# DeltaNet preparation by pairs of heads, in a new order of its parts, with the rotation's swapped rows copied inside SBUF

## The chip, the cores and the metric

The kernel runs on one NeuronCore of a Trainium2 chip. The metric is the device time of one execution in microseconds (us); the kernel before took 1733.33 us (median of 3 runs, 1732.29 to 1735.43).

## The reference: what is computed

One layer of a hybrid encoder is applied, with the same parameters, to a prompt of 1024 tokens and a sample of 256 tokens (1280 together, model width 1024). The normalized tokens are projected once (`h @ w_in`), and the columns go to two groups of heads:

```python
def _layer(...):
    h = _rmsnorm(x, norm_mix_pre)
    qkv_a, z_a, b_f, b_b, a_f, a_b, q_b, k_b, v_b = _split_cols(h @ w_in)
    o_a = _gated_deltanet(...)   # conv of 5 taps + SiLU, unit q/k, chunked delta rule, forward and backward
    o_b = _axial_gqa(...)        # per-head RMS norm of q/k, axial rotation, softmax attention
    x = x + _rmsnorm(concat([o_a, o_b]) @ w_out, norm_mix_post)
    f = square(relu(_rmsnorm(x, norm_mlp_pre) @ w_up)) @ w_down
    return x + _rmsnorm(f, norm_mlp_post)
```

For every chunk the delta rule solves a unit lower triangular system whose matrix is made of products of keys, a decay and a gate (`tri = I + strict(kk)`, `triangular_solve(tri, [v_beta, k_beta*exp(gc)])`). The kernel forms the inverses of these matrices itself, for 4 heads, 10 chunks of 128 tokens and 2 directions. In the attention group 4 query heads and 2 key heads are normalized and rotated (`x1*c - x2*s, x1*s + x2*c` on halves of 32 rows); 2 value heads aren't.

## The kernel before, in words

The program has four stages: norm and the z projection; the **preparation** of all heads; the scan over chunks together with attention; output projection and MLP. The change lies in the preparation. Each engine works in its own program order: PE (matmul), DVE, ACT, POOL, and SP, which here only issues DMAs.

The preparation is written as generators, one per part and head, and the string `ORDER` (L39 to L43) says which is advanced next; `next(parts[step_], None)` runs it to its next `yield` (L634 to L637). A scheduler then arranges the instructions of each engine by their place in this order and by what they depend on, and pools of buffers add dependences: a tile of a pool of one buffer can be written only when the readers of the tile before are done.

The parts are:

- **K** (`gdn_qk`): for one head the k projection and convolution, 10 transposes of k (`kt`, L459) of which ACT takes sums of squares and two scaled copies (`kn`, L464), and the same for q (`qt`, L473, without the copies). A projection (`proj_T`) is 72 matmuls `pt`: three for each of 8 slices of the depth (high by high, low by high, high by low; L367 to L369) over column groups of 512, 512 and 256 tokens. The convolution (`conv_proj`) has two steps on ACT, three long ones on DVE (L443), one on POOL (L444), a tanh on ACT (L445) and a last step on DVE (L446). The transposes need that last step.
- **V** (`gdn_v`): the same for v, with transposes `vt` (L502).
- **E** (`gdn_e`): for two chunks at a time, gate differences are built on PE in `pe` (L516, L522) from a tile `ER`, for direction 0 on POOL and for direction 1 on DVE (both L518); ACT takes the exponential `E` (L523); products of keys with keys and queries land in `pk` (L528), and DVE forms `A` (L529) and the system's matrix `C` (L531).
- **S** (`gdn_sub`): the 32x32 diagonal blocks of `C` are copied out (`Cc`, ACT L545), transposed (L547), written to DRAM and read back so that each of 80 partitions holds one block (`Rm`), which is inverted by 31 steps of elimination: a product `prod` (DVE L560), a sum into `Rm` (DVE L561), a memset (POOL L562). Once for each head.
- **L** (`gdn_lev`): `Rm` goes to DRAM (`r_d`, L569) and comes back as `Rc`; from the blocks' inverses the inverses of 64 and 128 rows are assembled in two levels of small matmuls with copies between (32x32: `ph` L589, `py` L596, `px` L601; 64x64: `ph` L618, `py` L625). The result is stored in `vis_d` (L629, L630), from where the scan loads it (`vis`, L652).
- **a** (`att_proj`): a projection of attention into `araw`. For q and k (a0 to a5) it is written to DRAM (`aqkv_d`, L391) and read back with its blocks of 32 rows swapped (`axw`, L394); 10 transposes (`at`, L400) give the sums of squares on ACT (`gj`, L376) for the norm; DVE multiplies `araw` and `axw` by the tables (L415, L416), POOL adds them (L417), and for a4 and a5 the keys are scaled by `prk`, a product on PE (L423, L426). The result goes to `arot_d` (L430). a6 and a7 are the values (`avn`, L406, L407). Attention reads `arot_d` as `ax` (L663).

In PSUM the preparation has eight banks: 3 for projections (`pt`), 2 shared by `pe` and `pk`, 1 for `kt`, `qt` and `vt`, 1 for the levels, and 1 for `at` and `prk`. The scan's first matmuls are `ps_s` (attention, L712) and `p` (L810).

## Time and profile before

| what | us |
|---|---|
| median of 3 runs (lowest to highest) | 1733.33 (1732.29 to 1735.43) |
| the profiled execution's own time | 1735.97 |
| span of its trace | 1734.2 |
| PE busy in it | 1622.7 (94%) |
| DVE, ACT, POOL busy | 1284.9, 851.7, 737.2 |
| start of attention's first product `ps_s`, of the scan's first `p` | 537.23, 541.73 |

The span is what the profiler recorded of one execution, 1.8 us less than that execution's own time. A row of waits names the instruction that waited, the one it waited for, the total, how often, and the longest. A row of instruction groups has the line, the engine, out<-in, the shapes and the count, then busy time and the mean length of one; behind the last bar stands the engine's idle time just ahead of the group. Where instructions overlap in an engine's pipeline, busy time divided by the count is less than the mean length. A row by windows gives busy time (and count) of each engine in a stretch of the span, then the granted clock of PE. The `order` rows below give only the sequence on one engine and say nothing of time.

### The profile page before, as it was taken

The page shows a single profiled execution, that of the slowest core. Times are in us where ns is not written, and L with a number is a line of the kernel's source. Part 1 is how long each engine was busy: PE and PEld are TensorE (multiplying, and loading weights), DVE is VectorE, ACT ScalarE, POOL GpSimd, SP SyncE. Part 2 cuts the span into 40 slices and gives each one's busy share as a digit, 9 for nine tenths or more (in the row PEclk, how much of TensorE's full clock was granted, in tenths as well). Part 3 has the DMA queues.
Part 4 walks back from the last instruction along what each step waited for, and adds up shares of the span by engine and source line. Part 5 has one row for each costly group of instructions (what it writes and reads, how often), then busy time and mean ns, then how long its engine had stood idle before and what let it go on. Part 6 is the DMA issues. An engine that isn't in the chain of part 4 may idle for free. (4 is left out here: it accounts for less than half of the span.)

```text
span 1734.2 us, 27996 instructions
## 1 busy us (share of the span) xinstructions
PE 1622.7 (94%) x9799; PEld 1386.8 (80%) x9799; DVE 1284.9 (74%) x2551; ACT 851.7 (49%) x1937; POOL 737.2 (43%) x656
## 2 busy tenths in 40 slices
PE   5999898988997999889998999999998999999997
PEld 4877676767775888658877999999988888888885
DVE  7545798997655788885659759555797878888777
ACT  4326566654344767674436546544554333333412
POOL 3212241312113434440103634644647677788762
PEclk9999999999998999999999999999999999999999
DMA  6213334545547866244334445444655444444234
GB/s 199 80 31 112 100 109 119 155 114 151 156 126 222 290 197 211 80 155 154 117 109 131 160 140 174 150 133 137 220 189 197 150 147 148 134 134 143 86 120 151
DMA packets 208779, 252.68 MB, mean 146 GB/s; under 512 B 35073, under 2 KB 163391, under 8 KB 208639
## 3 DMA queue, kind: packets, MB, share of 16 engines
q1 hardware_dynamic: 208495, 250.77, 45.8%
q8 instruction: 77, 1.26, 0.3%
q14 instruction: 63, 0.52, 0.1%
q0 software_dynamic: 144, 0.13, 0.0%
HBM read 159.75 MB, written 91.10 MB: 145 GB/s over the span
## 5 line engine op out<-in xcount | busy, mean ns | idle before, releaser
L1161 PE MATMUL pd<-mh,uhl 128*128 128x320 f32 x892 | 278.0, 312 | 6.8 <-DVE uhl L1152 6.7
L1160 PE MATMUL pd<-mh,uhl 128*128 128x320 f32 x892 | 276.5, 311 | 2.1 <-ACT uhl L1151 1.9
L1162 PE MATMUL pd<-ml,uhl 128*128 128x320 f32 x892 | 276.7, 310 | 0.0
L1304 DVE TENSOR_TENSOR acc<-acc,pd 128x512 f32<-128x512 f32 x330 | 207.0, 679 | 44.8 <-PE pd L1300 44.8
L1298 PE MATMUL pd<-dhi,fhi 128*128 128x512 f32 x490 | 193.0, 394 | 4.3 <-DVE acc L1306 4.3
L1299 PE MATMUL pd<-dl,fhi 128*128 128x512 f32 x490 | 192.8, 394 | 0.0
L1300 PE MATMUL pd<-dhi,flo 128*128 128x512 f32 x490 | 192.4, 393 | 0.0
L367 PE MATMUL pt<-h_hi,whi 128*128 128x512 f32 (+1 forms) x480 | 178.7, 372 | 0.0
L369 PE MATMUL pt<-h_hi,wlo 128*128 128x512 f32 (+1 forms) x480 | 178.4, 372 | 0.0
L368 PE MATMUL pt<-h_lo,whi 128*128 128x512 f32 (+1 forms) x480 | 178.2, 371 | 0.0
L1161 PEld LDWEIGHTS pd<-mh,uhl 128*128 128x128 f32 x892 | 168.8, 189 | 9.5 <-DVE uhl L1152 9.5
L1160 PEld LDWEIGHTS pd<-mh,uhl 128*128 128x128 f32 x892 | 168.5, 189 | 3.8 <-ACT uhl L1151 3.8
L1162 PEld LDWEIGHTS pd<-ml,uhl 128*128 128x128 f32 x892 | 168.6, 189 | 0.0
L1280 ACT CAST fhi<-fr 128x1280 fp32r<-128x1280 f32 x49 | 62.1, 1268 | 206.7 <-PE pd L1299 119.0
L80 POOL TENSOR_TENSOR dl<-dw,dhi 128x1024 fp32r<-128x1024 f32 x49 | 128.4, 2620 | 53.8 <-ACT dhi L79 53.3
L1205 POOL TENSOR_TENSOR s<-u,u 128x320 f32<-128x320 f32 x32 | 29.3, 915 | 224.4 <-ACT u L1170 219.5
L1152 DVE TENSOR_TENSOR uhl<-us,uhl 128x512 fp32r<-128x512 f32 x88 | 93.4, 1062 | 37.8 <-ACT uhl L1151 36.9
L727 POOL TENSOR_TENSOR P<-P,sm 128x512 f32<-128x512 f32 (+1 forms) x72 | 73.5, 1042 | 94.9 <-DVE sm L725 40.4
L1298 PEld LDWEIGHTS pd<-dhi,fhi 128*128 128x128 f32 x490 | 92.4, 188 | 25.8 <-DVE acc L1306 4.7
L1300 PEld LDWEIGHTS pd<-dhi,flo 128*128 128x128 f32 x490 | 92.3, 188 | 20.8
L1299 PEld LDWEIGHTS pd<-dl,fhi 128*128 128x128 f32 x490 | 92.4, 189 | 20.5
L1169 ACT ACTIVATE u<-u 128x320 f32<-128x320 f32 x128 | 60.1, 470 | 90.8 <-DVE u L1186 37.3
(359 smaller groups left out, 4128.5 us busy)
## 6 DMA issues: line engine op xcount, KB each, us to landing
fr<-r_d SPq DMA_DIRECT2D x49, 640.0 KB, 4.0
vis<-vis_d SPq DMA_DIRECT2D x64, 384.0 KB, 4.2
uraw<-in_w_up SPq DMA_DIRECT2D x22, 1024.0 KB, 5.4
r_d<-s SPq DMA_DIRECT2D x128, 160.0 KB, 1.8
r_d<-u SPq DMA_DIRECT2D x96, 160.0 KB, 1.9
dw<-in_w_down SPq DMA_DIRECT2D x28, 512.0 KB, 5.0
wraw<-in_w_in SPq DMA_DIRECT2D x48, 256.0 KB, 3.4
x<-in_x_prompt SPq DMA_DIRECT2D x16, 512.0 KB, 3.4
```

The source lines that it names most:

```text
L80: (V if leng is None else leng).tensor_tensor(lo, src, f32(hi), ALU.subtract)
L367: T.matmul(pm[:, :n], lhsT=whi, rhs=h_hi[:, k, t0:t0 + n], start=(k == 0), stop=False)
L368: T.matmul(pm[:, :n], lhsT=whi, rhs=h_lo[:, k, t0:t0 + n], start=False, stop=False)
L369: T.matmul(pm[:, :n], lhsT=wlo, rhs=h_hi[:, k, t0:t0 + n], start=False, stop=(k == KD - 1))
L1152: V.tensor_tensor(lo, ua[n][UP[i][0]], f32(hi), ALU.subtract)
L1160: T.matmul(pm, lhsT=w[0][:, k], rhs=mh[b, i][:, k], start=(k == 0), stop=False)
L1161: T.matmul(pm, lhsT=w[1][:, k], rhs=mh[b, i][:, k], start=False, stop=False)
L1162: T.matmul(pm, lhsT=w[0][:, k], rhs=ml[b, i][:, k], start=False, stop=(k == 3))
L1298: T.matmul(pm, lhsT=r[0][:, k, tk], rhs=w[0][:, k], start=(k == 0), stop=False)
L1299: T.matmul(pm, lhsT=r[0][:, k, tk], rhs=w[1][:, k], start=False, stop=False)
L1300: T.matmul(pm, lhsT=r[1][:, k, tk], rhs=w[0][:, k], start=False, stop=(k == Q - 1))
L1304: V.tensor_tensor(half(t, d), half(t, d), pm, ALU.add)
```

## The change

It has six parts, all in the preparation.

1. `ORDER` is another string. V0's projection stands behind K0's; the values a6 and a7 come early; a4 and a5 run while the second pair is eliminated; the levels L2 stand among a0 and a1 and L3 at the very end. There are more `yield`s in K, V, `att_proj` and S, so that the parts can be cut finer; in K the q projection comes before k's convolution.
2. S works on **two heads at once**: `Rm` is [80, 2, 32, 32], and each of the 31 steps has one product, one sum and one memset for both heads. `Rm` and `prod` have one buffer of double size each.
3. `ER` of direction 0 is four ACT copies with a scale instead of one POOL operation; `ER` and `A` have two buffers instead of one.
4. The PSUM banks of the transposes, levels, `at`, `prk` and now also `pk` are one shared pool `fx` of 3; `pe` keeps its 2 banks alone.
5. The swapped rows of `araw` are copied from SBUF to SBUF by four DMAs; the trip through `aqkv_d` goes. `axw` lies in the halves of a tile of the `qk` pool (two buffers), beside the tables in the other, so that both wait for K2's and K3's `qk` to be released.
6. `Cc` shares its buffer with `Rt`.

The diff, cut to its core:

```diff
 ORDER = (
-    "K0 K0 K0 K0 E0 E0 E0 E0 K1 E0 K1 S0 K1 K1 L0 E1 E1 V0 V0 E1 E1 L0 E1 K2 K2 K2 K2 E2 E2 E2 V1 E2 E2 "
...
-    "a2 a2 a3 a3 a7 a7"
+    "K0 K0 K0 V0 K0 K0 V0 E0 K1 E0 V0 E0 E0 K1 E0 K1 a6 K1 K1 a6 E1 E1 V1 E1 E1 E1 S0 K2 S0 V1 S0 K2 S0 V1 S0 K2 "
...
+    "V3 S1 a4 S1 a5 S1 a4 a5 a0 a5 L2 a0 a1 L2 a0 a1 a2 a1 a2 a3 a2 L3 a3 L3 a3"
...
-    tq_tile = b_tile("tq", 1)
-    iv_tile = b_tile("iv", 1)
-    at_tile = b_tile("at", 1)
+    tq_tile = iv_tile = at_tile = b_tile("fx", 3)
...
-            SP.dma_start(out=aqkv_d[j], in_=raw)
-            xw = tp_.tile([128, TOK], F32, tag="cy", name="axw", bufs=1)
+            xw = att["xw"][:, j % 2, 0:TOK]
             for b in range(4):
-                SP.dma_start(out=xw[b * 32:b * 32 + 32], in_=aqkv_d[j][(b ^ 1) * 32:(b ^ 1) * 32 + 32])
+                SP.dma_start(out=xw[b * 32:b * 32 + 32], in_=raw[(b ^ 1) * 32:(b ^ 1) * 32 + 32])
...
-    yield from conv_proj(4 + h, qk[:, 1])
+    pk_, pq_ = conv_proj(4 + h, qk[:, 1]), conv_proj(h, qk[:, 0])
+    next(pk_)
+    yield
+    next(pq_)
+    next(pk_, None)
+    yield
...
-                R = gp.tile([128, 2, 2, 128], F32R, tag="ER", name="ER", bufs=1)
-                (G if d == 0 else V).tensor_tensor(
...
+                R = gp.tile([128, 2, 2, 128], F32R, tag="ER", name="ER", bufs=2)
...
+                if d == 0:
+                    for i in range(2):
+                        for j in range(2):
+                            S.activation(R[:, i, j], incl[:, d], AF.Copy, scale=gd[:, i, j:j + 1])
...
-                pk = tr_tile("pk")
+                pk = tq_tile("pk")
...
-        Rm = gp.tile([80, 32, 32], F32, tag="Rm", name="Rm", bufs=2)
...
+        Rm = gp.tile([80, 2, 32, 32], F32, tag="Rm", name="Rm", bufs=1)
...
+            prod = gp.tile([80, 2, 256], F32, tag="prod", name="prod", bufs=1)
+            pv = prod[:, :, :p * n].rearrange("q h (j c) -> q h j c", j=p)
+            V.tensor_tensor(pv, Rm[:, :, p, 0:p][:, :, :, None].to_broadcast([80, 2, p, n]),
+                            Rm[:, :, p:p + 1, p:].to_broadcast([80, 2, p, n]), ALU.mult)
+            V.tensor_tensor(Rm[:, :, 0:p, p:], Rm[:, :, 0:p, p:], pv, ALU.add)
+            G.memset(Rm[:, :, p, 0:p], 0.0)
+            if p % 5 == 0:
+                yield
```

Three places show what this does to the sequence. The first is PE while E2 and E3 are built. In the kernel before, around the first group of E2 (`pe_2772`), with `pt` a projection's matmuls (the number behind a name is a buffer's):

```order
L516 MATMUL pe_2772<-nmask_839,identr_837 128x256
L522 MATMUL pe_2772<-ER_2774,strict_835 128x256 x2
L516 MATMUL pe_2772<-nmask_839,identr_837 128x256
L368 MATMUL pt_3754<-h_lo_100,whi_3744 128x512
L528 MATMUL pk_2785<-qk_2409 128x256
L459 MATMUL kt_3443<-ident_110,qk_3148 128x128 x2
L369 MATMUL pt_3754<-h_hi_99,wlo_3745 128x512
L522 MATMUL pe_2772<-ER_2779,strict_835 128x256 x2
```

and in the changed kernel, inside E2 and E3:

```order
L539 MATMUL pk_3591<-qk_2346 128x256
L533 MATMUL pe_3696<-ER_3706,strict_829 128x256
L539 MATMUL pk_3596<-qk_2346 128x256
L478 MATMUL qt_3603<-ident_104,qk_2843 128x128 x4
L522 MATMUL pe_3816<-nmask_833,identr_831 128x256
L533 MATMUL pe_3816<-ER_3818,strict_829 128x256 x2
L522 MATMUL pe_3816<-nmask_833,identr_831 128x256
L533 MATMUL pe_3816<-ER_3826,strict_829 128x256 x2
L478 MATMUL qt_3616<-ident_104,qk_2843 128x128 x4
L478 MATMUL qt_3629<-ident_104,qk_2843 128x128 x2
L539 MATMUL pk_3682<-qk_2346 128x256
```

Before, projections' matmuls stand between the parts of a group. Now, from `pk_3553` (six rows ahead of these) to the `at` transposes of a4, five groups of `pe`, 14 `pk` and 10 `qt` stand without a single `pt` between them. K3's `kt` have moved ahead of this, behind the levels of heads 0 and 1; one more group of `pe` and 30 `pt` stand between those and this place.

The second place is DVE where the rotated keys are scaled (`prk`), here of the first of a4 and a5. In the kernel before:

```order
L529 TENSOR_TENSOR A<-E,pk 128x256
L531 SCALAR_TENSOR_TENSOR C<-pk,sca,E 128x128 x2
L426 TENSOR_TENSOR araw<-araw,prk 128x512
L80 TENSOR_TENSOR wlo<-wraw,whi 128x512
L426 TENSOR_TENSOR araw<-araw,prk 128x512
L547 STREAM_TRANSPOSE Ct<-Cc 128x320
L426 TENSOR_TENSOR araw<-araw,prk 128x256
L415 SCALAR_TENSOR_TENSOR araw<-araw,nw,rope 128x1024
```

and in the changed one, where `80x2x...` is a step of the elimination of heads 2 and 3:

```order
L99 SCALAR_TENSOR_TENSOR rsa<-nat,nay 128x10
L575 TENSOR_TENSOR prod<-Rm 80x2x231
L577 TENSOR_TENSOR Rm<-Rm,prod 80x2x11x21
L425 TENSOR_TENSOR araw<-araw,prk 128x512
L575 TENSOR_TENSOR prod<-Rm 80x2x220
L425 TENSOR_TENSOR araw<-araw,prk 128x512
L577 TENSOR_TENSOR Rm<-Rm,prod 80x2x10x22
L425 TENSOR_TENSOR araw<-araw,prk 128x256
L575 TENSOR_TENSOR prod<-Rm 80x2x207
L415 SCALAR_TENSOR_TENSOR axw<-axw,nw,rope 128x1024
```

Before, E's operations were the neighbours, and the elimination of head 3 came later (`Ct`, which leads up to it, stands here). Now the norms and rotations of a4 and a5 lie between the steps of the elimination of heads 2 and 3, with one of its operations ahead of nearly each of theirs.

The third place is the end of the preparation. On PE before, with the last projection (a7), its transposes and attention's first products:

```order
L368 MATMUL pt<-h_lo,whi 128x256
L369 MATMUL pt<-h_hi,wlo 128x256
L400 MATMUL at<-ident,araw 128x128 x10
L712 MATMUL ps_s<-k_hi,q_hi 128x512
L713 MATMUL ps_s<-k_lo,q_hi 128x512
L714 MATMUL ps_s<-k_hi,q_lo 128x512
```

and in the changed kernel, behind a3's projection and the 32x32 levels of head 3:

```order
L398 MATMUL at<-ident,araw 128x128 x10
L634 MATMUL ph_5615<-X_1011,C 64x64 x10
L634 MATMUL ph_5627<-X_1011,C 64x64 x10
L641 MATMUL py_5639<-C,H_5614 64x64 x10
L641 MATMUL py_5652<-C,H_5614 64x64 x10
L826 MATMUL p_5839<-vis 128x128 x2
L833 MATMUL p_5845<-vt,vis 128x128 x2
L826 MATMUL p_5854<-vis 128x128 x2
L842 MATMUL p_5845<-vt,vis 128x128 x2
L833 MATMUL p_5860<-vt,vis 128x128 x2
L728 MATMUL ps_s<-k_hi,q_hi 128x512
L729 MATMUL ps_s<-k_lo,q_hi 128x512
```

On SP before:

```order
L407 DMA arot_d<-avn 128x512
L407 DMA arot_d<-avn 128x256
L663 DMA ax<-arot_d 128x256
L663 DMA ax<-arot_d 128x512
L430 DMA arot_d<-araw 128x1280
L652 DMA vis<-vis_d 128x512
L652 DMA vis<-vis_d 128x384
```

and in the changed kernel (the last `arot_d<-araw` is a3's rotation, `vis_d<-C` are head 3's inverses):

```order
L429 DMA arot_d<-araw 128x1280
L679 DMA ax<-arot_d 128x512
L645 DMA vis_d<-C 1280x1x128
L646 DMA vis_d<-C 1280x1x128
L429 DMA arot_d<-araw 128x1280
L668 DMA vis<-vis_d 128x512
L668 DMA vis<-vis_d 128x384
L668 DMA vis<-vis_d 128x128
```

Before, all levels were done ahead of the last projections (L3's matmuls had 36 `pt` among them), and the last work was a7's transposes. Now the levels of head 3 and the norm and rotation of a3 stand behind the last projection with no `pt` left; the scan's loads `vis` stand behind both on SP's queue, and on PE the scan's `p` stands ahead of attention's `ps_s`. L2 stands in the same way, without a `pt` among its matmuls, between a2's projection and a3's.

More of the change, by code (lines that the diff above doesn't have):

```diff
@@ L111, in build @@
     z_d = dr.tile([TOK, 512], F32, name="z_d")
-    aqkv_d = [dr.tile([128, TOK], F32, name=f"aqkv{j}_d") for j in range(6)]
     arot_d = [dr.tile([128, TOK], F32, name=f"arot{j}_d") for j in range(8)]
@@ L380, in att_proj @@
     def att_proj(j):
-        if not att:
+        if not att and j < 6:
             rope = gp.tile([128, 2, 1282], F32, tag="qk", name="rope", bufs=2)[:, :, 0:1024]
             SP.dma_start(out=rope, in_=I["c_rope"])
-            att[0] = rope
-        rope = att[0]
+            att["rope"] = rope
+            att["xw"] = gp.tile([128, 2, 1282], F32, tag="qk", name="axw", bufs=2)
+        rope = att.get("rope")
         c = (2064 + j * 128, 2576 + (j - 4) * 128, 2832 + (j - 6) * 128)[max(0, j - 2) // 2]
@@ L467, in gdn_qk @@
         yield
-        yield from conv_proj(h, qk[:, 0])
+        next(pq_, None)
+        yield
         for t0 in range(0, NT, 4):
@@ L496, in gdn_v @@
         yield from conv_proj(8 + h, vT)
+        yield
         irk = irks[h]
@@ L537, in gdn_e, with gdn_sub @@
         Cs[h] = C
[L539 to L555 removed]
+    def gdn_sub(pair):
+        Rm = gp.tile([80, 2, 32, 32], F32, tag="Rm", name="Rm", bufs=1)
+        for i in range(2):
+            h = 2 * pair + i
+            C = Cs[h]
+            Cc = gp.tile([128, 2, NT, 32], F32, tag="Rt", name="Cc", bufs=1)
+            for b in range(4):
+                bs = slice(32 * b, 32 * b + 32)
+                S.mul(Cc[bs], C[bs, :, :, bs].rearrange("p t d c -> p d t c"), -1.0)
+            Ct = gp.tile([128, NT, 32], F32, tag="Ct", name="Ct", bufs=1)
+            V.transpose(Ct.rearrange("p t c -> p (t c)"), Cc[:, 0].rearrange("p t c -> p (t c)"))
+            c_d = dr.tile([128, 2, NT, 32], F32, tag="c_d", name="c_d", bufs=2)
+            SP.dma_start(out=c_d[:, 0], in_=Ct)
+            SP.dma_start(out=c_d[:, 1], in_=Cc[:, 1])
+            for b in range(4):
+                SP.dma_start(out=Rm[20 * b:20 * b + 20, i], in_=c_d[32 * b:32 * b + 32].rearrange("j d t i -> (d t) j i"))
+            Rms[h] = Rm[:, i]
+        G.memset(Rm.rearrange("p h a b -> p h (a b)")[:, :, 0:1024:33], 1.0)
+        yield
```

31 lines of the change are left out of this document (6 added, 25 removed), and 1 row of the table ORDER.

## The prediction

> **What bounds the kernel now.** I first read the busy shares of the profile's first part: PE is busy for 94% of the span, but the change touches only the preparation, so what counts is read there. The table of windows cuts that stage by time; its columns are each engine's busy time, then the granted PE clock:
>
> ```profile
> core 0: us, PE busy (x) PEld busy (x) DVE busy (x) ACT busy (x) POOL busy (x), PEclk, DMA share, GB/s
> 112.00:212.00 100.00, 88.90 (x459) 72.28 (x460) 62.78 (x111) 60.07 (x170) 24.54 (x29) 0.98 0.37 102
> 212.00:312.00 100.00, 91.97 (x719) 74.13 (x719) 87.52 (x187) 66.37 (x177) 27.79 (x70) 0.95 0.45 121
> 312.00:392.00 80.00, 71.50 (x621) 56.83 (x620) 77.12 (x180) 43.29 (x114) 21.81 (x52) 1.00 0.46 124
> 392.00:492.00 100.00, 92.23 (x736) 74.75 (x735) 70.19 (x191) 40.21 (x131) 19.47 (x45) 0.97 0.49 140
> 492.00:542.00 50.00, 40.45 (x434) 31.80 (x433) 19.01 (x52) 16.96 (x48) 7.12 (x3) 0.83 0.58 177
> 501.00:509.00 8.00, 8.00 (x98) 6.61 (x96) 1.12 (x3) 2.48 (x5) 0.00 (x0) 0.57 0.01 2
> 532.00:542.00 10.00, 4.64 (x11) 3.24 (x12) 3.44 (x7) 1.97 (x4) 1.27 (x1) 0.50 0.93 302
> ```
>
> PE is the engine that sets the pace. The first five rows cover 430 us, PE is busy in 385.05 of them, and so idles 44.95. DVE is nearly its equal only from 312 to 392 (77.12 of 80). What a new order can win is this idle time, so I next asked what PE waited for, by its waits in the first 280 us and in the rest:
>
> ```profile
> PE vt L502 <- DVE vT L446: 7.1, 3, 2.5
> PE pe L516 <- DVE C L531: 5.9, 5, 2.5
> PE qt L473 <- DVE qk L446: 3.6, 2, 2.2
> PE pk L528 <- DVE prod L560: 2.3, 1, 2.3
> PE kt L459 <- DVE qk L446: 1.9, 1, 1.9
> ```
>
> ```profile
> PE ps_s L712 <- ACT q_hi L79: 6.2, 1, 6.2
> PE prk L423 <- DVE araw L426: 4.1, 2, 2.6
> PE pe L516 <- DVE C L531: 2.3, 1, 2.3
> PE prk L423 <- DVE rsa L98: 0.8, 1, 0.8
> ```
>
> Each `vt`, `qt` or `kt` waits because its transposes stand close behind a convolution that isn't done; each `pe` waits for a bank whose last user was a `pk` that DVE still had to read.
>
> **The change part by part.** (a) *Waits that go.* Transposes now stand a projection or more behind their convolution, and `pk` leaves the two banks of `pe`. That addresses 7.1 + 3.6 + 1.9 = 12.6 us and 5.9 + 2.3 = 8.2 us, with the 2.3 of `pk` 23.1 in all. Not all stays won: K3's `kt` and its neighbours share three banks with everything else, and each reader there can be late in the same way. I count 18 us won, with ends at 23 (nothing replaced) and 12 (half replaced).
>
> (b) *Elimination by pairs.* The rows of its products and sums:
>
> ```profile
> L561 DVE TENSOR_TENSOR Rm<-Rm,prod 80x31 f32<-80x31 f32 (+15 forms) x124 | 51.6, 416 | 2.3
> L560 DVE TENSOR_TENSOR prod<-Rm 80x31 f32<-80x31 f32 (+15 forms) x124 | 43.4, 350 | 4.0 <-POOL Rm L555 1.9
> L560 DVE TENSOR_TENSOR prod<-Rm 80x31 f32<-80x31 f32 x8 | 1.5, 183 | 2.0 <-POOL Rm L555 1.9
> L560 DVE TENSOR_TENSOR prod<-Rm 80x256 f32<-80x256 f32 x4 | 1.7, 418 | 0.1
> ```
>
> From 31 to 256 elements the product grows from 183 to 418 ns, 1.04 ns for an element, which leaves 183 - 32 = 151 ns that don't depend on size. 248 operations become 124 of twice the size, so 124 x 151 ns = 18.7 us of DVE go, of 95.0. The Trainium skill, page "Perfetto Trace Analysis", section "Optimizing Scalar/DVE Operations", puts the overhead of a DVE operation on SBUF at about 60 ns of engine time and says that the profiled latency is about twice that, since half overlaps with the next instruction; by it 124 x 60 ns = 7.4 us would go, an estimate. The rows' 151 ns are over twice that; each step here needs the one before, so little of a step can overlap, and the sum keeps to the rows.
>
> What does it bring PE? Where PE waits for something else, nothing. Only from 312 to 392 is DVE nearly full, and PE idles there for 80 - 71.50 = 8.5 us. So the gain lies between 0 and 8.5; I take 3, near zero, because no elimination step is among what PE waits for, but for the single 2.3 us already used.
>
> (c) *The stretch of E2 and E3 with no projection in it* (first place of the order). The rows that price it:
>
> ```profile
> L518 POOL TENSOR_TENSOR ER<-incl,gr 128x512 fp32r<-128x512 f32 x20 | 29.3, 1463 | 70.6 <-PE pe L522 70.6
> L518 DVE TENSOR_TENSOR ER<-incl,gr 128x512 fp32r<-128x512 f32 x20 | 15.6, 782 | 9.4 <-PE pe L522 9.3
> L464 ACT ACTIVATE kn<-kt,cum 128x128 f32<-128x128 f32 x80 | 22.6, 397 | 0.2 <-DMA vis_d<-kn 0.2
> L523 ACT ACTIVATE E<-pe 128x512 f32<-128x512 f32 x20 | 12.1, 603 | 18.1 <-PE pe L522 18.1
> L529 DVE TENSOR_TENSOR A<-E,pk 128x256 f32<-128x256 f32 x40 | 16.5, 412 | 12.4 <-ACT E L523 7.7 <-PE pk L528 2.6 <-ACT cy L440 2.1
> L531 DVE SCALAR_TENSOR_TENSOR C<-pk,sca,E 128x128 f32<-128x128 f32 x80 | 24.3, 341 | 0.4 <-DMA vis_d<-C 0.4
> L516 PE MATMUL pe<-nmask,identr 128*128 128x256 f32 x40 | 12.9, 322 | 8.3 <-DVE C L531 8.2
> L522 PE MATMUL pe<-ER,strict 128*128 128x256 f32 x80 | 18.1, 307 | 1.4 <-DVE ER L518 1.4
> L528 PE MATMUL pk<-qk 128*128 128x256 f32 x80 | 26.1, 413 | 3.2 <-DVE prod L560 2.3 <-ACT E L523 0.7
> L473 PE MATMUL qt<-ident,qk 128*128 128x128 f32 x40 | 7.3, 299 | 4.4 <-DVE qk L446 3.6 <-ACT gj L376 0.6
> ```
>
> A scaled copy of 128x128 on ACT takes 22.6 / 80 = 0.28 us where they run back to back (`kn`). So the four for one `ER` cost 1.13 us, and POOL loses 29.3 us of work that delayed no one by more than 1.4. PE's own work in the stretch is 10 x 0.32 + 20 x 0.226 + 14 x 0.326 + 10 x 0.18 = 14.1 us. DVE's is 5 x 0.78 + 14 x (0.41 + 2 x 0.30) = 18.1 us. A group taken serially is 1.13 (copies) + 0.45 (PE) + 0.78 (DVE's `ER`) + 0.45 (PE) + 0.60 (`E`) + 0.41 (`pk`) + 1.09 (`A`, two `C`) = 4.9 us, and five are 24.5. The exposed idle time is then between 18.1 - 14.1 = 4 and 24.5 - 14.1 = 10 us, up to 14 with the sixth group ahead of it, which has 30 short `pt` as cover. I take 10: two banks of `pe`, and `ER`, `A` and `C` of neighbouring groups queued on one DVE, are nearer to the serial end.
>
> (d) *The rotations of a4 and a5 between elimination steps* (second place). By the slope of (b) a step of 252 elements for two heads takes 151 + 504 x 1.04 = 675 ns. From a4's sums to its `prk` about eleven steps stand between, 7.4 us, and as much again for a5; `prk` needs `rsa`, and PE works in order, so the projection behind `prk` waits for it too. Before, this place cost 4.1 + 0.8 = 4.9. The ends are -4.9 (the projection ahead covers all) and 2 x 7.4 - 4.9 = +9.9; I take +6: only 24 and 32 `pt` stand between the transposes and `prk`, and at 0.11 us from start to start for 256 columns (the first two rows of the last fence of this part) and twice that for 512, they cover 3 to 7 us of each wait that also holds the sums, the norm and the `wlo` of other projections. The swap inside SBUF is costed at nothing:
>
> ```profile
> L416 DVE SCALAR_TENSOR_TENSOR axw<-axw,nw,rope 128x1024 f32<-128x1024 f32 (+1 forms) x12 | 10.2, 878 | 3.7 <-DMA axw<-aqkv_d 3.7
> ```
>
> The round trip was waited for once, 3.7 us, by DVE and not by PE; that is the most it gives back. Its copies now also wait for K2's and K3's `qk` to be free; behind them on SP stand the loads `wraw` of the next projection. If these come late they cost PE what the rotation costs, so (d)'s upper end holds that too. One buffer each for `Rm` and `prod`, and `Cc` in `Rt`'s, are costed at nothing: steps on DVE follow each other anyway, and L0 and L1 have read the first pair's `Rm` before the second is loaded; were they late, S1 would wait and with it (e).
>
> (e) *L2 with no projection among its matmuls* and (f) *the end*. The levels' first and last matmuls and the stores behind them:
>
> ```profile
> L589 PE MATMUL ph<-Rt,C x160: 191/191/212, 287.2 to 496.1; 32*32 32x32 f32 x160
> L625 PE MATMUL py<-C,H x160: 218/218/268, 297.0 to 512.3; 64*64 64x64 f32 x160
> L629 SPq DMA_DIRECT2D vis_d<-C x4: 523/542/1029, 301.4 to 513.5; - x4
> ```
>
> ```profile
> 527.78 0.28 PE L368 MATMUL pt<-h_lo,whi 128*128 128x256 f32 x1
> 527.89 0.28 PE L369 MATMUL pt<-h_hi,wlo 128*128 128x256 f32 x1
> ...
> 530.63 0.44 PE L400 MATMUL at<-ident,araw 128*128 128x128 f32 x2 [0.68 <-ACT avn L406]
> 537.23 0.80 PE L712 MATMUL ps_s<-k_hi,q_hi 128*128 128x512 f32 x1 [6.17 <-ACT q_hi L79]
> 541.73 0.85 PE L810 MATMUL p<-vis 128*128 128x128 f32 x4
> ```
>
> Head 0 takes 301.4 - 287.2 = 14.2 us from its first level matmul to its store; head 3, from its last first-level matmul to its store, 513.5 - 496.1 = 17.4. In between lie copies on ACT and DVE, for which PE now has nothing to do. For L2 I take 5 us of idle (a third of 14.2; ends 2 and 9, that is half of 17.4). At the end, before, `ps_s` starts 6.2 us late and `p` 541.73 - 531.07 = 10.7 after the last transposes. Now L3's chain of 14.2 to 17.4 stands there, and a store and load through SP behind it, behind a3's rotation on the same queue; against this, L3 no longer stands in the middle, where at a clock of 0.57 the 8 us from 501 to 509 lost 8 x 0.43 = 3.4. The ends are 14.2 - 10.7 - 3.4 = 0 and 17.4 - 10.7 = 6.7 with half as much again for the rotation and the loads behind it, 10; I take their middle, +5.
>
> The sum against the profiled execution is -18 - 3 + 10 + 6 + 5 + 5 = +5 us, 1735.97 + 5 = 1741. That execution lay 2.6 us above the median, so in the measure of the median it is 1733.3 + 5 = 1738.
>
> **The rivals.** About 0.2%, 3.5 us, is what a measurement of this kernel can tell from no change.
>
> *Faster.* The waits of (a) go in full (-23), DVE's saving is worth PE's idle time where DVE is full (-8.5), and the shared banks let PE take matmuls from elsewhere, so that (c) costs 4; with (d), (e) and (f) at half, 8, that is -19.5, or 1714. For it speaks that 23.1 of 45 us idle lie in waits that the order takes apart; against it, that the order shows no cover in (c), (e) and (f). It decides if the stretch of E2 and E3 shows less than about 5 us of PE waits. Chance 0.28.
>
> *No change.* Half of (a) comes back at the shared banks (-12), and (c) to (f) cost as much: 1733. The profile would then show about 45 us of PE idle time, in other rows. Chance 0.15.
>
> *Slower by much.* PE's clock falls where PE waits. The last two rows of windows show it at 0.57 and 0.50, the second behind a wait of 6.2. Through the stretch of (c), at half clock, PE's 14.1 us of work take up to 14.1 more; nearly all of it counts if PE is the serial link there, little if it idles anyway. With the sum's +5 that gives +18, about 1752. It decides from a granted clock below about 0.7 in that stretch. Chance 0.15. The Trainium skill, page "TensorE: Matmul & The Clock Gate", section "Part 1: The HAM clock gate", says that an idle window of about 3.4 us puts PE back to half clock, and as long a busy one lifts it; the trace agrees at 532 to 542 (0.50 behind 6.2 us), and the rule speaks against any order that gathers waits in one place.
>
> **How the numbers follow.** The forecast of 1738 has the remaining chance of 0.42; its terms' ends, taken as independent (half-widths of about 5.5, 4, 5, 7, 3.5 and 5), give about 13 either way, 1725 to 1751. The range reaches a little past the faster rival's 1714, to 1712, and to the slower one's 1752. Faster by over 0.2%: 0.28 and 0.08 of the forecast's lower part, 0.36. Within: 0.13 of the no-change case and 0.07 of the forecast, 0.20. Slower: 0.27 of the forecast, 0.15, and 0.02 of the rest, 0.44.
>
> **What would show it.** Step (a) is right if the waits of `vt`, `qt` and `kt` for L446 fall from 12.6 to under 6 us and `pe` waits for `C` no more. (b): the 124 operations sum to 95.0 - 18.7 = 76 us. (c): a stretch of 25 us or so without `pt`, in which PE is busy for about 14 and waits for ACT or DVE. (d): `prk` or the projection around it waits over 10 us. (e), (f): L2's and L3's matmuls show waits for copies, and the first `p` starts 14 us or more after the last `pt` with head 3's stores just ahead. The forecast is wrong if `p` starts earlier than in the kernel before, at 541.73, by more than 3.5 us, or later by more than 15.

## The result, and the profile after

The changed kernel takes 1752.85 us (median; 1750.26 to 1755.26) against 1732.81 of the kernel before beside it: a ratio of 1.0115, interval 1.0095 to 1.0135, so 20 us slower. The profiled execution took 1753.38 with a span of 1751.6 (before 1735.97 and 1734.2). The forecast was 1738 and slower by 5; the time lies just above the range's 1752.

Read as before, the busy shares first, and then the windows (busy time of each engine, then the granted clock):

```profile
PE 1620.2 (92%) x9799; PEld 1394.0 (80%) x9799; DVE 1257.9 (72%) x2427; ACT 868.5 (50%) x2017; POOL 697.1 (40%) x572
```

```profile
112.00:212.00 100.00, 99.26 (x538) 83.91 (x537) 61.77 (x115) 74.08 (x220) 15.05 (x21) 0.98 0.42 116
212.00:312.00 100.00, 93.64 (x499) 78.17 (x498) 83.22 (x131) 60.71 (x151) 20.93 (x43) 0.98 0.36 97
312.00:392.00 80.00, 69.90 (x848) 55.63 (x847) 48.41 (x114) 47.18 (x137) 3.65 (x10) 0.96 0.47 124
392.00:492.00 100.00, 76.44 (x593) 62.87 (x591) 66.25 (x143) 33.45 (x99) 12.71 (x35) 0.91 0.39 105
492.00:542.00 50.00, 35.25 (x477) 30.00 (x473) 31.78 (x86) 27.22 (x109) 10.95 (x4) 0.77 0.47 131
373.00:398.00 25.00, 18.01 (x84) 12.88 (x85) 19.77 (x70) 19.93 (x67) 0.00 (x0) 0.93 0.70 203
```

The first three stages got better: PE idles 0.74 + 6.36 + 10.10 = 17.2 us there, where it idled 11.1 + 8.03 + 8.5 = 27.6. The gain of 10.4 is then given back and more: from 392 to 542 PE idles 23.56 + 14.75 = 38.3, against 7.77 + 9.55 = 17.3, at a lower clock (0.91 and 0.77, before 0.97 and 0.83). So the question is what happened behind 392. PE's waits from 100 to 570 us (total, times, longest):

```profile
PE at L398 <- DVE araw L425: 11.2, 1, 11.2
PE p L826 <- DMA vis<-vis_d: 11.1, 2, 10.3
PE at L398 <- ACT araw L368: 4.2, 1, 4.2
PE pk L539 <- DVE C L542: 4.0, 2, 3.2
PE px L617 <- issue: 3.8, 3, 1.6
PE pt L365 <- ACT araw L368: 3.7, 1, 3.7
...
PE qt L478 <- DVE qk L445: 2.2, 1, 2.2
...
PE prk L422 <- DVE rsa L99: 1.7, 1, 1.7
PE vt L508 <- DVE vT L445: 1.7, 1, 1.7
```

The waits of the early stages (`vt`, `qt`, `kt`, `pe` for `C`) have all but gone. The two largest are new: one wait of 11.2 us while the second pair is eliminated, one of 10.3 at the scan's first product. Both, and the waits near the first, on PE's timeline (start, duration, and in brackets the idle time ahead with what ended it):

```profile
444.96 2.78 PE L398 MATMUL at<-ident,araw 128*128 128x128 f32 x10 [11.22 <-DVE araw L425]
451.41 0.80 PE L365 MATMUL pt<-h_hi,whi 128*128 128x512 f32 x1 [3.67 <-ACT araw L368]
...
463.26 2.50 PE L422 MATMUL prk<-ident,rsa 128*128 128x128 f32 x20 [1.72 <-DVE rsa L99]
...
546.54 0.77 PE L826 MATMUL p<-vis 128*128 128x128 f32 x2 [10.34 <-DMA vis<-vis_d]
...
553.06 0.55 PE L728 MATMUL ps_s<-k_hi,q_hi 128*128 128x512 f32 x1
```

And DVE's timeline ahead of it:

```profile
415.37 0.69 DVE L81 TENSOR_TENSOR wlo<-wraw,whi 128x512 fp32r<-128x512 f32 x1 [4.06 <-ACT whi L80]
416.79 0.69 DVE L81 TENSOR_TENSOR wlo<-wraw,whi 128x512 fp32r<-128x512 f32 x1 [0.72 <-ACT whi L80]
424.19 0.17 DVE L89 TENSOR_SCALAR nax<-ssa 128x10 f32<-128x10 f32 x1 [6.71 <-ACT gj L374]
...
426.53 0.17 DVE L99 SCALAR_TENSOR_TENSOR rsa<-nat,nay 128x10 f32<-128x10 f32 x1
426.80 0.22 DVE L575 TENSOR_TENSOR prod<-Rm 80x62 f32<-80x62 f32 x1
...
435.60 1.27 DVE L414 SCALAR_TENSOR_TENSOR araw<-araw,nw,rope 128x1024 f32<-128x1024 f32 x1
...
441.09 3.22 DVE L577 TENSOR_TENSOR Rm<-Rm,prod 80x480 f32<-80x480 f32 x1
444.23 0.67 DVE L425 TENSOR_TENSOR araw<-araw,prk 128x512 f32<-128x512 f32 x1
```

Here a4's norm (L89 to L99) stands *ahead* of the second elimination in DVE's program. It waits 6.71 us for the squares that ACT sums from a4's transposes. Only when it is done does the elimination start, at 426.80. a4's rotation (from L414 on) then stands in turn behind and between elimination steps, and the scaling by `prk` (L425), which frees the bank that a5's transposes (`at`) want, comes at 444.23, behind POOL's add for this rotation (440.62 to 443.79, shown in the last section) and the step at 441.09.

### The profile page after: what moved, and what is told of

It reads as the page before. It is cut to its first block, busy times and chain, and to the rows that moved or that the text cites. A ratio compares the mean times of both kernels' runs of the same rounds, so it can differ in the third digit from the quotient of the medians.

```text
span 1751.6 us, 27869 instructions
## 1 busy us (share of the span) xinstructions
PE 1620.2 (92%) x9799; PEld 1394.0 (80%) x9799; DVE 1257.9 (72%) x2427; ACT 868.5 (50%) x2017; POOL 697.1 (40%) x572
## 5 line engine op out<-in xcount | busy, mean ns | idle before, releaser
L1177 PEld LDWEIGHTS pd<-mh,uhl 128*128 128x128 f32 x892 | 168.3, 189 | 11.3 <-DVE uhl L1168 11.2
L367 PE MATMUL pt<-h_hi,wlo 128*128 128x512 f32 (+1 forms) x480 | 174.4, 364 | 0.9 <-DVE wlo L81 0.9
L81 POOL TENSOR_TENSOR dl<-dw,dhi 128x1024 fp32r<-128x1024 f32 x49 | 128.6, 2624 | 54.4 <-ACT dhi L80 53.8
L365 PEld LDWEIGHTS pt<-h_hi,whi 128*128 128x128 f32 x480 | 92.0, 192 | 18.1 <-ACT araw L368 4.1
```

Source lines behind the costliest of these rows:

```text
L81: (V if leng is None else leng).tensor_tensor(lo, src, f32(hi), ALU.subtract)
L365: T.matmul(pm[:, :n], lhsT=whi, rhs=h_hi[:, k, t0:t0 + n], start=(k == 0), stop=False)
L367: T.matmul(pm[:, :n], lhsT=wlo, rhs=h_hi[:, k, t0:t0 + n], start=False, stop=(k == KD - 1))
L1177: T.matmul(pm, lhsT=w[1][:, k], rhs=mh[b, i][:, k], start=False, stop=False)
```

## Experiments

Two events mark how far the late part is: the start of attention (first `ps_s`) and of the scan (first `p`). The last projection matmul (`pt`) starts at 522.1 in the changed kernel and at 527.9 before, but then the changed kernel still has levels of head 3 to do, and the kernel before hasn't; `ps_s` starts at 553.1 against 537.2, and `p` at 546.5 against 541.7. The first matmul of the next stage (`pd`) starts at 923.5 against 907.6, 15.9 later; the spans differ by 17.4.

Before the runs are compared, one thing has to be known. The scheduler arranges the whole program anew for each edit, so PE's order can also turn in the stage of scan and attention, which no edit touches. By the sequence of names on PE from the earlier of the two marks to the first `pd`, the versions fall into groups with the very same sequence, and the time from that mark to `pd` goes with the group (versions by the headings below):

| PE's order in this stage | first | us from the earlier mark to `pd` |
|---|---|---|
| kernel before; "elimination first"; "L3 still last" | `ps_s` | 370.3; 369.6; 370.1 |
| changed kernel; `ER` back on POOL; `Rc` on POOL's queue; the same with "elimination first" | `p` | 376.9; 377.2; 377.0; 378.5 |
| old sequence; late part reordered; a3's store on POOL's queue | `ps_s` | 377.2; 377.1; 379.4 |
| the three with L3 among the projections | `ps_s` | 378.1; 379.0; 378.7 |
| third buffer with step 10 and own banks; with step 18 and `Rc` on POOL's queue | `ps_s` | 378.0; 377.3 |
| third buffer with step 18; elimination head by head | `ps_s` | 385.1; 387.5 |

The three versions that are left have orders of their own: 372.5 (third buffer with step 10), 383.8 (`at` in its own banks) and 376.6 (the kernel before with `ER` on ACT). `ps_s` starts 14 to 24 us ahead of `p` in the last group and with own banks, and 4 to 13 in the other versions where it is first. So a difference between two runs is the price of what was edited only where this order is the same in both. Each trace is of one execution, and some lie off the median: that of own banks took 1752.88, that of `Rc` on POOL's queue 1760.92, that with the third buffer besides 1734.63.

**The old sequence with the new operations.** The string is cut as the new parts need it, in the order of the kernel before:

```diff
-    "K0 K0 K0 V0 K0 K0 V0 E0 K1 E0 V0 E0 E0 K1 E0 K1 a6 K1 K1 a6 E1 E1 V1 E1 E1 E1 S0 K2 S0 V1 S0 K2 S0 V1 S0 K2 "
+    "K0 K0 K0 K0 K0 E0 E0 E0 E0 K1 E0 K1 K1 K1 K1 E1 E1 V0 V0 V0 E1 E1 E1 S0 S0 S0 S0 K2 S0 S0 S0 S0 L0 K2 K2 L0 "
...
```

> All new parts (pairs, ER on ACT, shared banks, copies inside SBUF), but put in the sequence of the kernel before: each part's extra yields are run through at once, the values a6 stand among E3, a7 last, L2 and L3 ahead of a2 and a3. Theory 'late order' (the loss of 20 us lies in the rotations among the elimination, L2 without a projection, and the end, which are matters of the order): 1725 to 1740 us, with the waits of vt, qt and kt for the convolution back (over 8 us in all). Rival 'parts' (the new forms of the operations themselves cost the 20 us): about 1750, whatever the order.

Measured: 1766.87 (1.0186, 1.0159 to 1.0214), slower than either theory said. PE waits 16.6 us for `wlo` and 13.5 for the `at` bank. So the new sequence is not the loss as a whole: with these operations it is 14 us better than this version of the old one.

**`at` in banks of its own** (those of `pe`; only a6 and a7 keep the shared ones):

```diff
-            tp = at_tile("at")
+            tp = (tr_tile if j < 6 else at_tile)("at")
```

> The changed kernel with one edit: the transposes at of a0 to a5 go to the two banks of pe instead of the shared three, so that prk can no longer hold the banks they need. Theory 'banks': the waits of at for DVE L425 (11.2 us) and behind it go and the levels of head 2 find projections between: 1732 to 1743. Rival 'elimination sets the end' (the second elimination ends on DVE at 477.5 and everything behind L2 waits for it): PE only waits later, 1748 to 1753.

Measured: 1746.82 (1.007, 1.0047 to 1.0092), 6 less, between the two expectations. PE's waits show where they went:

```profile
PE ph L605 <- DVE Rt L592: 12.9, 3, 12.5
PE prk L422 <- DVE araw L425: 10.4, 1, 10.4
```

The wait of `at` is gone; the next instruction that needs DVE waits 10.4 instead, and the levels of head 3 another 12.5. In this trace the bank only chose who waits for DVE.

**Elimination head by head**, where the pair stands:

```diff
-            V.tensor_tensor(pv, Rm[:, :, p, 0:p][:, :, :, None].to_broadcast([80, 2, p, n]),
...
+            for i in range(2):
+                R1 = Rm[:, i]
...
```

> The changed kernel with the elimination of the two heads of a pair one after the other (248 operations of single size on DVE instead of 124 of double size); Rm, loads and yields as in the changed kernel. The prediction's reading (pairing is worth 3 us, at most 8.5): 1753 to 1761. Rival 'elimination sets the end' (the second pair's 62 steps lie on the critical path): 9 us more for the second pair alone, 1762 or above. A shift below 1753 would mean that pairing does not help where it stands.

Measured: 1763.06 (1.0166, 1.014 to 1.0192), about 10 us over the changed kernel and in the rival's window. But the last product of the second elimination starts only 5.0 us later (482.3 against 477.3), and PE's order turned, with 24 us between `ps_s` and `p`. So the 10 us aren't the price of pairing alone.

**`ER` of direction 0 back on POOL:**

```diff
-                if d == 0:
-                    for i in range(2):
-                        for j in range(2):
-                            S.activation(R[:, i, j], incl[:, d], AF.Copy, scale=gd[:, i, j:j + 1])
...
+                (G if d == 0 else V).tensor_tensor(R, incl[:, d][:, None, None, :].to_broadcast([128, 2, 2, 128]),
```

> The changed kernel with ER of direction 0 on POOL again (one operation of 1.46 us) in place of four ACT copies; two buffers of ER stay. Prediction's reading (the stretch of E2 and E3 costs 10 us because ACT, PE and DVE work serially there): ACT's copies of 1.13 us become 1.46 on POOL, so 1751 to 1756. Rival 'parts': ACT's 80 copies are what delays the E stretch and other ACT work, 1745 or less.

Measured: 1763.44 (1.0166, 1.0138 to 1.0193), slower than either reading said. PE's order from `p` on is the changed kernel's here, so the copies on ACT, with what they shift in the preparation, are worth about 10 us in this order.

**The late part in another order** (a0 and a1 during the elimination, a4 and a5 after it, a7 last; `at` in its own banks as above):

```diff
-    "V3 S1 a4 S1 a5 S1 a4 a5 a0 a5 L2 a0 a1 L2 a0 a1 a2 a1 a2 a3 a2 L3 a3 L3 a3"
+    "S1 a0 S1 a1 S1 a0 a0 a1 a1 a4 a4 a4 a5 L2 a5 L2 a5 a2 L3 a2 a2 L3 a3 a3 a3 a7 a7"
```

> The changed kernel up to E3, then another late part: at of a0 to a5 in the banks of pe (as e2), a0 and a1 instead of a4 and a5 beside the second elimination, which starts ahead of their norms on DVE; L2 and L3 with projections among their matmuls; the value a7 last, as in the kernel before. Theory 'late order' (early part 23 us better than before, late part 40 worse): 1715 to 1728. Rival 'parts and DVE' (the second elimination on DVE paces the late part in any order): 1740 or more.

Measured: 1765.41 (1.0201, 1.0181 to 1.0222): the theory missed, and the time lies in the rival's window. PE's timeline, and the SP queue's:

```profile
455.56 1.97 PE L398 MATMUL at<-ident,araw 128*128 128x128 f32 x8 [24.40 <-ACT araw L368]
```

```profile
451.44 0.34 SPq L429 DMA_DIRECT2D arot_d<-araw  x1
```

`araw` has two buffers. One is free only when a rotation is stored, here at 451.44, and the rotation lies among the elimination's steps again. By this reading any rotated projection put there would meet the same limit.

**L3 still last, with a7 ahead of a4** (own banks too):

```diff
-    "V3 S1 a4 S1 a5 S1 a4 a5 a0 a5 L2 a0 a1 L2 a0 a1 a2 a1 a2 a3 a2 L3 a3 L3 a3"
+    "V3 S1 a7 a4 S1 a5 S1 a4 a4 a5 a5 a0 a0 a0 a1 L2 a1 L2 a1 a2 L3 a2 L3 a2 a3 a3 a3"
```

> As e5 (banks, a7 behind V3, L2 with projections among its matmuls), but a4 and a5 stay beside the second elimination and L3 stays last, behind a3's projection. Theory 'late order' by its parts: the end's 17 us stay, the rotations' 16 go in part, so 1733 to 1745, about 12 to 17 above e5. If the end costs little (the prediction's 5 us), it lies within 6 us of e5.

Measured: 1747.06 (1.0087): the same as own banks alone. `prk` waits 10.1 for DVE as there. Neither expectation held: it lies 18 us below the version before it, not 12 to 17 above it.

**The kernel before, with `ER` on ACT and two buffers:**

```diff
-                R = gp.tile([128, 2, 2, 128], F32R, tag="ER", name="ER", bufs=1)
-                (G if d == 0 else V).tensor_tensor(
...
+                R = gp.tile([128, 2, 2, 128], F32R, tag="ER", name="ER", bufs=2)
...
+                            S.activation(R[:, i, j], incl[:, d], AF.Copy, scale=gd[:, i, j:j + 1])
```

> The kernel before with one part of the change: ER of direction 0 as four ACT copies instead of one POOL operation, two buffers of ER. If e4's 10 us is a property of the operation (POOL's 1.46 us on the way to each pe), 1722 to 1729 here too; if it comes from how it stands in the changed order, 1731 to 1738, no difference that can be told from the kernel before.

Measured: 1768.42 (1.0219, 1.0199 to 1.0238), 36 us slower and outside both expectations. The same copies that gain 10 in the new order cost 36 in the old one, with waits of `vt` 8.5, `qt` for `gj` 7.8 and for `qk` 7.4. The edit also rearranges the instructions, so 36 isn't the price of the copies; operations and order can't be priced apart here.

**a3's store on POOL's queue** instead of SP's:

```diff
-        SP.dma_start(out=arot_d[j], in_=raw)
+        (SP if j != 3 else G).dma_start(out=arot_d[j], in_=raw)
```

> The changed kernel with one DMA moved: a3's rotated result is stored by POOL's queue instead of SP's, so that the scan's loads vis do not stand behind it. In the changed kernel SP waits from 538.6 to 542.1 for it, with head 3's inverses stored at 537.8. Theory 'queue': 3 us less, about 1750. Rival: p waits for other loads that come as late, no change, 1752 to 1754.

Measured: 1754.03 (1.0129): no gain, as the rival said. The wait of `p` goes, `ps_s` comes first on PE, and waits 9.4 us for `q_hi`.

**Elimination first.** a4's norm is held behind step 18 of the second elimination in DVE's program (the steps count down from 31, so this is the 14th):

```diff
-        rsqrt(gp, rs, ssa[:, j], NT, 1.0 / 128, "na")
+        with tc.issue_after(elim[1, 18].ins) if j in (4,) else nullcontext():
+            rsqrt(gp, rs, ssa[:, j], NT, 1.0 / 128, "na")
```

> The changed kernel with one more order: on DVE a4's norm may be issued only behind the 14th of the 31 steps of the second elimination. In the changed kernel that elimination's data and its first memset are there at 411, but DVE idles until 424.2, because a4's norm stands ahead of it and waits for ACT's sums. Theory 'DVE order': elimination, prk and the banks behind it come 13 us earlier, 1736 to 1744. Rival 'buffers' (a4's and a5's araw hold both buffers and the next projection can't be copied out, so that a later rotation costs what an earlier elimination brings): 1749 to 1758.

Measured: 1740.42 (1.0046, 1.003 to 1.0062), 12.4 less, inside what the theory of DVE's order said. DVE's timeline, and two of PE's waits:

```profile
415.77 0.69 DVE L81 TENSOR_TENSOR wlo<-wraw,whi 128x512 fp32r<-128x512 f32 x1 [0.72 <-ACT whi L80]
416.38 0.21 DVE L577 TENSOR_TENSOR prod<-Rm 80x62 f32<-80x62 f32 x1
```

```profile
PE prk L423 <- DVE rsa L99: 20.8, 2, 17.2
PE ps_s L730 <- ACT q_hi L80: 8.5, 1, 8.5
```

The elimination starts 10.4 us earlier, directly behind the two `wlo` (L81) that still stand ahead of it, and its last product starts at 463.3 instead of 477.3. PE waits longer at this place than it did (17.2 in one piece), and still the kernel is faster: `ps_s`, the later of the two marks in the changed kernel, starts at 541.0, 12.1 us earlier, and `p`, now the later, at 545.5, 1.1 earlier.

Yet this isn't the price of the norm's place. PE's order behind the preparation turned with the edit: `ps_s` is first again, and the sequence is that of the kernel before. PE enters the stage 5.6 us earlier (541.0 instead of 546.5), and the stage is 7.3 us shorter (369.6 instead of 376.9). A pair of runs below differs by the held norm too, but has the changed kernel's order in both: there it gains nothing (1753.08 without, 1755.75 with). And the run above, with `ps_s` first (in an order of another group) and the late elimination, gains nothing either. So the late elimination is shown, and that this edit gains 12.4 us; how much of that the earlier elimination brings is not.

**L3 among the projections**, upon that:

```diff
-    "V3 S1 a4 S1 a5 S1 a4 a5 a0 a5 L2 a0 a1 L2 a0 a1 a2 a1 a2 a3 a2 L3 a3 L3 a3"
+    "a4 S1 V3 S1 a4 S1 a5 S1 a4 a5 a0 a5 L2 a0 a1 L2 a0 a1 L3 a2 a1 L3 a2 a3 a2 a3 a3"
```

> e9 with L3 moved ahead of a3 in the sequence of the parts, so that 38 of a3's matmuls stand behind L3's and only a3's transposes at the end. Theory 'end' (head 3's levels and rotation behind the last projection cost about 17 us more than the end before, of which the levels are 10 to 14): 10 to 14 us below e9. The prediction's size of the end (5 us): 0 to 5 below e9.

Measured: 1751.7 (1.011), 11 slower than with L3 last, which refutes the theory of the end as I had put it. `ps_s` starts at 542.5, hardly later, but `p` at 555.3: now 12.7 us of attention's products stand ahead of the scan's on PE, where it was 4.5.

**The same with `at` in its own banks**, and **with the levels of both heads one behind the other** (`L2 L2 L3` ahead of a0, `L3` behind it):

> e10 with the transposes at of a0 to a5 in the banks of pe, as in e2. If waits for banks are still left in e10, 3 to 8 us below e10; if elimination and araw buffers set the pace, within 3 of e10. A time below 1730 would be below both kernels.

> e11 with L2 and L3 directly one behind the other, ahead of a1's transposes, so that a2 and a3 follow both and only a3's transposes are last. Theory 'end' again: if what counts is that no level stands behind the last projection, within 4 us of e11; if the levels need projections among their matmuls (L3 has none here), 5 to 10 above e11.

Measured: 1750.36 (1.0099) and 1751.8 (1.012); `p` at 554.0 and 552.5. Neither helps: the first lies within 3 us of the version it was built on, as was expected if banks don't set the pace, the second within 4 of the first.

**A third buffer for `araw`**, upon "elimination first", with the norm behind step 10, and then behind step 18:

```diff
-        raw = tp_.tile([128, TOK], F32, tag="cp", name="araw", bufs=2)
+        raw = (gp.tile([128, 1282], F32, tag="vT", name="araw", bufs=1)[:, 0:TOK] if j in (0, 3)
+               else tp_.tile([128, TOK], F32, tag="cp", name="araw", bufs=2))
```

> e9 with a third buffer for araw (a0's and a3's lie in vT's, which is free behind V3) and a4's norm behind the 22nd of the 31 elimination steps instead of the 14th; 127 matmuls of a5 and a0 now stand ahead of prk. In e9 PE waited 17.2 us for rsa at prk. Theory 'buffers' (with two of them nothing can be projected while a rotation waits for the elimination): 12 to 18 us below e9, 1722 to 1729. Rival 'DVE's pace' (elimination, rotations and levels end as late as before, PE only waits in another place): within 4 us of e9, 1737 to 1744.

> e13 with a4's norm behind the 14th step, as in e9; 91 matmuls stand ahead of prk. Theory 'buffers': between e9 and e13, 1724 to 1732. 'DVE's pace': as e9.

Measured: 1742.46 (1.0054, 1.0032 to 1.0076) and 1740.06 (1.0046, 1.0019 to 1.0072): no gain over 1740.42, both in the window of 'DVE's pace'. But the second moved `ps_s` to 524.4, 16.6 us earlier, with `p` at 547.2. The third buffer of the first with `at` in its own banks:

> e13 with the transposes at of a0 to a5 in the banks of pe. L2 has projections among its matmuls, L3 not. If banks held by prk still cost something in e13, 2 to 6 below it; if not, within 3 of it.

Measured: 1749.59 (1.012), 7 us worse and outside both expectations.

**Head 3's `Rc` loads on POOL's queue.** In the changed kernel head 3's levels begin some 30 us behind head 2's (`Rt` at 517.2 and 486.9). Its SP queue shows a candidate:

```profile
492.17 2.55 SPq L589 DMA_DIRECT2D Rc<-r_d  x3
...
506.57 2.48 SPq L392 DMA_DIRECT2D axw<-araw  x4
509.16 0.52 SPq L429 DMA_DIRECT2D arot_d<-araw  x1
509.72 0.46 SPq L589 DMA_DIRECT2D Rc<-r_d  x1
...
537.15 0.58 SPq L645 DMA_DIRECT2D vis_d<-C  x1
...
543.60 2.72 SPq L668 DMA_DIRECT2D vis<-vis_d  x6
```

Three of the four loads are issued at 492; the fourth stands behind a rotation's swap copies and its store, and goes at 509.72. The edit, on the changed kernel, on "elimination first", and on the third buffer with step 18:

```diff
-            SP.dma_start(out=Rc[bs].rearrange("j d t i -> j (d t) i"), in_=r_d[20 * b:20 * b + 20].rearrange("n j i -> j n i"))
+            (G if h == 3 else SP).dma_start(out=Rc[bs].rearrange("j d t i -> j (d t) i"), in_=r_d[20 * b:20 * b + 20].rearrange("n j i -> j n i"))
```

> The changed kernel, with head 3's four loads of `Rc` issued by POOL's queue instead of SP's; nothing else is edited. SP-queue theory (the start of the scan is set by the fourth `Rc` load of head 3, which stands on SP behind the swap copies and the rotation stores of a2): head 3's first level starts about 15 us earlier (near 502 instead of 517), the first `p` by 5 to 12 us, and the time falls to 1740-1747. Rival (PE's own queue and the levels' matmuls set it, or POOL's queue is as late because its adds for the rotations stand between the loads): the time stays within 4 us of 1753.

> As elimination_first (a4's norm held until step 18 of the second elimination), with head 3's `Rc` loads on POOL's queue. SP-queue theory: the two gains lie at different places and add: 1728-1736, and the first `p` near 533. Rival (the start of attention, `ps_s`, takes over, or POOL's queue is as late): within 4 us of the 1740 that elimination_first took.

> As third_buffer_mid (a third buffer for araw, `ps_s` started at 524 but `p` only at 547), with head 3's `Rc` loads on POOL's queue. SP-queue theory: here only `p` was late, so it gains most: `p` near 530 and 1722-1732, faster than the kernel before. Rival (head 3's levels are late for another reason: PE's order, DVE's `Rt`, or the `vis` loads): `p` stays past 542 and the time within 4 us of 1740.

Measured: 1753.08 (1.011, 1.0079 to 1.0142), 1755.75 (1.0139, 1.0096 to 1.0181) and 1738.72 (1.003, 1.0012 to 1.0048). The first and the third lie in their rivals' windows, the second in neither. POOL's timeline in the first:

```profile
497.25 1.46 POOL L589 DMA_DIRECT2D Rc<-r_d  x2 [16.08 <-PE px L617]
500.42 2.89 POOL L416 TENSOR_TENSOR araw<-araw,axw 128x1280 f32<-128x1280 f32 x1 [1.71 <-issue]
503.26 1.36 POOL L589 DMA_DIRECT2D Rc<-r_d  x2
507.99 2.47 POOL L416 TENSOR_TENSOR araw<-araw,axw 128x1280 f32<-128x1280 f32 x1 [3.37 <-issue]
```

The loads wait 16.08 us on POOL for head 2's levels, and the rotations' adds behind them begin at 500.42 and 507.99 instead of 496.00 and 503.12. In this execution the second elimination had already started 3.5 us later (430.3 against 426.8), so of the 4 to 5 us about 1 is left for the loads. Head 3's first level is 6 us earlier (the transpose that makes `Rt` starts at 510.9, not 517.2), and `p` isn't: it waits 11.7 us for `vis`, whose loads stand on SP behind a3's rotation (stored at 546.6), while head 3's inverses are stored from 540.9 on. So the fourth `Rc` load didn't set the start of the scan.

The second has PE's order from `p` on as the first, and its elimination starts 10.1 us earlier than there; this is the pair named above, and no gain shows. Against "elimination first" it loses 15 us, and its trace shows a later start of the stage (550.0 against 541.0, of which 3.8 are there at the elimination's start) and a longer stage (378.5 against 369.6).

In the third the theory's mechanism shows: that transpose starts at 494.9 instead of 515.9, and PE starts both late stages early. Before and after, here "third buffer with step 18" and this version:

```profile
516.85 0.26 PE L608 MATMUL ph<-Rt,C 32*32 32x32 f32 x2 [15.62 <-DVE Rt L595]
```

```profile
528.79 0.80 PE L731 MATMUL ps_s<-k_hi,q_hi 128*128 128x512 f32 x1 [14.54 <-ACT q_hi L80]
...
533.29 1.05 PE L829 MATMUL p<-vis 128*128 128x128 f32 x4
```

Yet the time is 1738.72 against its base's 1740.06, in the rival's window, not 1722 to 1732. The first `pd` starts at 906.1 against 909.5, so of the 13.9 us that `p` gained most is lost. Two things in the traces say where. The wait of 15.62 us for `Rt` is gone, but one of 14.54 for `q_hi` stands in its place: in the base PE did attention's products from 524.4 on while `p` was late. And PE's order turned: from `p` this stage takes 372.8 us, as in the other version with this order (373.8), where it took 362.3 in its base. Why one order is longer than another stays open. It is the best of the changed versions, and it doesn't beat the kernel before.

## Why the prediction was wrong

The direction was right, the size was not: 20 us instead of 5. By its steps:

**(a), waits that go (-18): right.** Of the 23.1 us counted there, `qt`, `vt` and `pk` still show 2.2 + 1.7 + 4.0 = 7.9, a gain of 15.2 (forecast 12 to 23). (a), (b) and (c) together were to bring -18 - 3 + 10 = -11; the three first windows, where they lie, show -10.4.

**(b), pairing (-3): the work saved on DVE was right, what it brings the kernel stays open.** The rows of the paired steps:

```profile
L577 DVE TENSOR_TENSOR Rm<-Rm,prod 80x62 f32<-80x62 f32 (+15 forms) x62 | 37.5, 604 | 1.1
L575 DVE TENSOR_TENSOR prod<-Rm 80x62 f32<-80x62 f32 (+15 forms) x62 | 32.2, 519 | 1.2
```

They sum to 69.7 us, so 25.3 of 95.0 went; the forecast was 18.7, to 76. But some steps took far longer than the others of their shape (the last section shows one), and there were more of them before. With the median of each shape in place of its single times the sums are 83.5 and 64.4, and the difference is 19.0: the forecast's 151 ns for each operation fit. The Trainium skill's 60 ns an operation ("Perfetto Trace Analysis", "Optimizing Scalar/DVE Operations") made 7.4 of it; the trace doesn't bear that out here, where each step needs the one before. The version head by head was about 10 us slower, but with another order on PE.

**(c), the stretch without projections (+10): right.** From 373 to 398 PE idles 25 - 18.01 = 7.0 us (ends 4 and 14). A scaled copy took longer than its `kn` neighbour:

```profile
L528 ACT ACTIVATE ER<-incl,gr 128x128 fp32r<-128x128 f32 x80 | 29.1, 414 | 0.2 <-PE pe L533 0.2
```

29.1 / 80 = 0.36 us, not 0.28, which PE hardly felt. The granted clock there is 0.93. So the rival *slower by much*, which named 1752 and came out near the measured time, is wrong in its cause: it decides from a clock below 0.7 in that stretch. Its sentence that the clock falls where PE waits doesn't fit the first of its two rows either: from 501 to 509 PE is busy for 8.00 of 8.00 us, at 0.57.

**(d), the rotations of a4 and a5 among the elimination (+6): too small, and half of the mechanism missed.** At this place PE now waits 11.2 + 3.7 + 1.7 = 16.6 us, against 4.9: +11.7, over the upper end of 9.9. I had priced eleven steps between a4's sums and its `prk`, that is, what the elimination does to the rotation. What the rotation does to the elimination was left out: a4's norm, ahead of it in DVE's program, held it back for 10.4 us. The order was there to be read before the run; I read it at `prk`, and not at the head of the elimination. What this delay costs the kernel isn't shown: holding the norm gained 12.4 us in one pair of runs, in which PE's order turned too, and nothing in the other, in which it didn't.

**(e), L2 (+5): right within its ends.** Around L2 PE waits 1.59 for `Rt` and some 2.9 in short pieces (0.2 to 1.1 us each). With the 4.2 for `araw` at 505.6, 6 us behind L2's last matmul, it is about 8.7, within (e)'s 2 to 9.

**(f), the end (+5): the step that failed.** The sum measured the end at `p`, 10.7 us after the last transposes, and credited that to the old kernel. But its own rows show no wait of `p` there: PE had been at attention's products from 537.23 on, after 6.17 us of idle time. In the changed kernel `p` starts 4.8 us later (546.5 against 541.7), as good as the forecast's 5, and the sign I had named came too (`p` 14 us or more after the last `pt`: 24.4); the kernel is 20 us slower all the same. Measured where PE enters the stage, at the earlier of `ps_s` and `p`, the end comes 9.3 us later (546.5 against 537.2). And the stage behind was put at nothing, without a reason, though the order ahead of the prediction shows that `p` now stands ahead of `ps_s`: it takes 376.9 us instead of 370.3, another 6.6. The two make the 15.9 us by which `pd` is later; 1.5 more come behind it, and 2.6 of the 20 are the profiled executions' distance from their medians.

How far this is shown: that the stage's length goes with PE's order holds over all groups of the table, with quite different preparations in a group. The 9.3 us are located by PE's waits (behind 392, up to 542, it idles 21.0 us more, where (d), (e) and (f) were to cost 16), but no run prices them one by one. The fourth `Rc` load behind a rotation on SP wasn't in the sum, though the order shows it; the runs with POOL's queue show that it alone doesn't set the time.

All of the last three terms came out near or over their upper ends. I had taken them "as independent" for the range, with a half-width of 13; added straight, the half-widths make 30. That they hang on one chain, and so err together, is argued and not shown.

## What to carry to other kernels

Price a change of order at the point where the next stage begins on the engine that sets the pace, not at one instruction of that stage: here `p` moved by 4.8 us as forecast, and the stage began 9.3 later. Then compare that engine's order behind this point in both kernels. A scheduler that arranges the whole program can turn it far from the edit, and a stage that nobody had touched took from 369.6 to 387.5 us by its order. The same comparison belongs ahead of every experiment: a run prices its edit only where the rest of the order stood still.

When a change puts a long chain on one in-order engine among other work, read what stands *ahead of its first instruction* and what that waits for, not only what stands within it: a norm of 13 short operations held this chain back by 10.4 us. Whether the delay costs anything is a question of its own.
